# Making the low part of every fourth weight tile by an accumulating transfer instead of a VectorE subtraction

## The chip, the cores and the metric

The kernel runs on one core of a Trainium2 chip. The metric is the device time of one execution in microseconds (us), as the median of several runs; less is better. The engines are named as the profile names them: PE is TensorE (matrix products; PEld are its weight loads), DVE is VectorE, ACT is ScalarE, POOL is GpSimd, SP is SyncE, which here only issues transfers. A "q" behind an engine's name means its instruction sequencer. Besides these, 16 DMA engines move data between HBM and the on-chip memory.

## The reference

One layer of an encoder over 256 positions of width 2048, all in float32. Cut to its matrix products:

```python
hn = rms_norm(h, g_mix_pre);  u = hn @ w_in                     # 2048 x 5120
q, k, v, xr, yg = split(u)
attn = neighborhood_attention(q, k, v, rpb)
rec = rglru_bidirectional(xr, ...) * gelu(yg)
mixed = concat([rms_norm(attn), rms_norm(rec)]) @ w_out         # 2048 x 2048
h = h + rms_norm(mixed, g_mix_post)
fn = rms_norm(h, g_ffn_pre)
ff = (silu(fn @ w_ffn_gate) * (fn @ w_ffn_up)) @ w_ffn_down     # 2048 x 5632, twice, and back
h = h + rms_norm(ff, g_ffn_post)
gate = sigmoid(rms_norm(h, g_ple_pre) @ w_ple_gate)             # 2048 x 2048
h = h + rms_norm(gate * (p @ w_ple_proj), g_ple_post)           # 256 x 2048
```

## The kernel before

**Split products.** Each float32 operand is held as two numbers of the narrower type fp32r (`F32R`): a high part, which is the value rounded, and a low part, which is the value less its high part. A product is three matmuls into one float32 accumulator: high by high, high by weight-low, low by weight-high (lines 390, 391, 392 in `products`).

**Weight tiles.** All weights are cut into 412 tiles of 128 partitions by 2 by 512 float32 numbers (512 KB each, 4 KB per partition), listed in `tiles` in the order of use: 80 for `w_in` (0 to 79), then `w_out`, two of `w_ple_proj`, the feed-forward weights, two more of `w_ple_proj`, and 32 for `w_ple_gate`. Each tile takes twelve matmuls of 512 columns on PE. A tile goes through four steps, numbered by tile `i`:

- `load_stream` (line 339): SP issues the transfer of the raw tile from HBM into `wr`. There are four such buffers (`R_BUFS`), used in turn, so tile `i` takes the buffer of tile `i-4`, and its transfer waits until that buffer was last read.
- `hi_stream` (line 362): ACT copies `wr` into `wh`, which rounds it. `wh` and `wl` have four buffers each (`W_BUFS`), so the copy of tile `i` waits for the last matmul of tile `i-4`.
- `lo_stream` (line 372): DVE writes `wl = wr - wh`. It is the last reader of `wr`.
- `products` (lines 390 to 392): PE uses `wh` in the first matmul of the tile and `wl` in the second.

The first tile is loaded in two halves, and the last eight tiles keep their buffers for a second pass, four of them in buffers of their own (`bw`).

**The order of the work.** Every engine runs its instructions in the order in which the program issues them. That order comes from a planner (`Plan`): each stream is a generator that yields the engine it needs next and an estimated cost, and the planner keeps a clock for each engine and issues whatever can start first, in time before PE needs it. `act(n)`, `dve(n)` and `dma(kb)` are such costs; `take` and `give` count buffers, and an `Event` holds the planned time at which something is done. The planner's clocks only set the order. On the chip each instruction waits by semaphores for what it reads and for the buffer it writes.

POOL issues no transfer in this kernel: it only clears buffers and makes constants.

Of the kernel before, what the change touches and what calls it, by code (L numbers as in the profile page):

```python
# [12 lines left out]
AF = mybir.ActivationFunctionType  # L13
ALU = mybir.AluOpType
# [13 lines left out]
N = 512  # L28
# [25 lines left out]
R_BUFS = 4  # L54
SM_BUFS = 4
LATE = 0.8


class Event:
# [5 lines left out]
class Task:  # L65
    def __init__(self, gen, ready, late):
        self.gen, self.ready, self.sure, self.late, self.op = gen, ready, ready, late, None


class Plan:  # L70
# [11 lines left out]
    MARGIN = 0.4  # L82

    def __init__(self, **slots):
        self.clk = {"act": 0.0, "dve": 0.0, "pe": 0.0, "dma": 0.0}
        self.free = {k: [0.0] * n for k, n in slots.items()}
        self.tables = None
        self.tasks = []
        self.now = 0.0
# [97 lines left out]
def act(n, tables=COPY, take=None, give=None):  # L187
    return ("act", 0.15 + 0.00082 * n, tables, take, give)


def dve(n, take=None, give=None):
    return ("dve", 0.08 + 0.00104 * n, None, take, give)


def pe(cost, take=None, give=None):
    return ("pe", cost, None, take, give)


def dma(kb, take=None):
# [4 lines left out]
def layer(ctx: ExitStack, tc: tile.TileContext, a: dict, out: bass.AP):  # L204
    nc = tc.nc
# [4 lines left out]
    plan = Plan(wr=R_BUFS, w=W_BUFS, sm=SM_BUFS, ev=1, mid=2, bt=2)  # L210

    def f32(t):
        return t.bitcast(F32)
# [41 lines left out]
    def transposed(e, b0):  # L255

        yield pe(0.44, take="sm")
        tr = bank("tr")
        for b in range(2):
            for t in range(NT):  # L260
                sl = slice((b0 + b) * P, (b0 + b + 1) * P)
                nc.tensor.transpose(tr[:, b, t * P : (t + 1) * P], e[:, t, sl], ident)  # L262
        return tr
# [13 lines left out]
    def done(event):  # L277
        event.t = plan.now
# [32 lines left out]
    tiles = []  # L311
# [7 lines left out]

    raws, his, los = {}, {}, {}  # L320
    ev_raw, ev_hi, ev_lo = {}, {}, {}
    extra_loads = {}
    big_w = {}

    def pieces(i):

        return [slice(0, 1), slice(1, 2)] if i == 0 else [slice(0, 2)]
# [16 lines left out]
    def lateness(at):  # L344

        return LATE if at[0] - at_pe[0] >= 2 else -LATE

    def hi_stream():
        for i in range(len(tiles)):
            at_hi[0] = i  # L350
            for j in pieces(i):
                n = j.stop - j.start
                yield ev_raw[i, j.stop]
                if i in big_w:
                    yield big_w[i][2]
                yield act(n * N, take=None if j.start or i in big_w else "w")
                if i in big_w:
                    his[i], los[i] = big_w[i][0](), big_w[i][1]()
                elif not j.start:
                    his[i] = wp.tile([P, 2, N], F32R, tag="wh", name="wh")  # L360
                    los[i] = wp.tile([P, 2, N], F32R, tag="wl", name="wl")
                nc.scalar.copy(his[i][:, j, :], raws[i][:, j, :])  # L362
                done(ev_hi[i, j.stop])

    def lo_stream():
        for i in range(len(tiles)):
            at_lo[0] = i
            for j in pieces(i):
                n = j.stop - j.start
                yield ev_hi[i, j.stop]  # L370
                yield dve(n * N, give="wr" if j.stop == 2 else None)
                nc.vector.tensor_tensor(  # L372
                    out=los[i][:, j, :], in0=raws[i][:, j, :], in1=f32(his[i][:, j, :]),
                    op=ALU.subtract,
                )
                done(ev_lo[i, j.stop])
            raws.pop(i)
# [82 lines left out]
    def make_hT(odd):  # L460
        for k in range(odd, KD // 2, 2):
            for j in range(2):
                b = 2 * k + j
                yield ev_xs[b]
                yield from gained_split(
                    hT_hi[:, b, :], hT_lo[:, b, :], xs[k][:, j, :], col("g_mix_pre", b)
                )
                done(hT.ev[b])
# [4 lines left out]
    def norm_x():  # L473
        ss = const.tile([P, NT, 2], F32, name="ss_x")
        for i in range(2 * NT):
            t, c = i // 2, i % 2
            v = xn[t][:, c * DA : (c + 1) * DA]
            yield ev_xn[i]
            yield act(DA)
            nc.scalar.activation(v, v, AF.Square, accum_out=ss[:, t, c : c + 1])  # L480
        tot = const.tile([P, NT], F32, name="tot_x")
        yield dve(64)
        nc.vector.tensor_reduce(out=tot, in_=ss, op=ALU.add, axis=AX.X)
        yield from rstd_of(tot, D, rstd_x, const.tile([P, NT], F32, name="rt_x"))
        done(ev_x)
# [137 lines left out]
    def rec_unit(b0, xp):  # L623
# [24 lines left out]
        for i, (dst, bn) in enumerate(((r, "b_rg_a"), (ig, "b_rg_i"))):  # L648
            pg = [None] * 2
            for z in range(2):  # L650
                yield pe(0.66, take="sm")
                pg[z] = bank("pg")
                for c in range(2):
                    w = 4 * z + 2 * i + c
                    mm3(pg[z][:, c, :], gh[:, w, :], gl[:, w, :], xch[:, c, :], xcl[:, c, :],
                        True, True)
            for z in range(2):
                for c in range(2):
                    yield act(S, SIG, give="sm" if c else None)
                    nc.scalar.activation(  # L660
                        dst[:, z, c, :], pg[z][:, c, :], AF.Sigmoid, bias=col(bn, z * 8 + b0 + c)
                    )
                if i:
                    plan.add(gate_input(z, gated[z]), plan.now)
# [55 lines left out]
    def group_rstd(ss, name):  # L720

        yield pe(0.44, take="sm")
        pb = bank(f"pb_{name}")
        nc.tensor.matmul(pb[:, 0, :], ones, ss, start=True, stop=True)
        rb = const.tile([P, S], F32, name=f"rb_{name}")
        yield act(S, SQRT, give="sm")
        nc.scalar.activation(rb, pb[:, 0, :], AF.Sqrt, bias=eps, scale=1.0 / DA)
        yield dve(S)
        nc.vector.reciprocal(rb, rb)
        return rb  # L730
# [592 lines left out]
    for i in range(len(tiles)):  # L1323
        for j in pieces(i):
            for ev in (ev_raw, ev_hi, ev_lo):
                ev[i, j.stop] = Event()
    i0 = segs[-1][-1]
    keep.update(range(i0, i0 + 8))
    bw = {}
# [12 lines left out]

    plan.add(load_stream())
    plan.add(hi_stream(), late=lambda: lateness(at_hi))
    plan.add(lo_stream(), late=lambda: lateness(at_lo))
    plan.add(make_hT(0), late=-2 * LATE)
    plan.add(make_hT(1), late=-2 * LATE)
    plan.add(norm_x())
# [77 lines left out]
```

## Time and profile before

| | us |
|---|---|
| median of 2 runs (1197.97 and 1198.37) | 1198.17 |
| span of the profiled execution, first to last instruction | 1195.1 |
| PE busy within the span | 1176.7 |
| DVE busy | 695.1 |
| ACT busy | 635.0 |
| POOL busy | 1.6 |

The profile is of one execution. What lies around its span isn't in the trace: its own time is not listed apart from the runs', whose median stands 3.1 us above the span. The granted TensorE clock of the core was 0.997 of full speed. Matmuls are pipelined, so the duration of one (0.39 us) is longer than the distance from one to the next, and "busy" is the time in which at least one is under way.

A line of a group reads: source line, engine, operation, tiles written and read, shape, count, then busy time, mean duration of one in ns, idle time of the engine just before these instructions, and what ended that idle time. A line of the timeline reads: start in us from the span's start, duration in us, engine, line, operation, tiles.

### The profile page before, as it was taken

Reading aid. Unit: us, or ns where it says so; the run is one execution under the profiler, and the core shown is the slowest. Engines: PE = TensorE matmul, PEld = TensorE weight load, DVE = VectorE, ACT = ScalarE, POOL = GpSimd, SP = SyncE. Lnnn points to the kernel's source line nnn. Section 1 sums busy time; section 2 is a strip of 40 time slices with the busy share of each in tenths; the row PEclk is TensorE's granted clock in tenths of the full one; section 3 lists DMA queues with packets and bytes.
Section 4 is the critical chain, followed back from the end, with each engine's and each line's share of the span. In section 5 each row is a group of like instructions: output and inputs, shape, how many; then the busy total and the mean of one; then the engine's idle time right before and its main releaser. Section 6 shows DMA issues by size and latency. Waiting matters only on the chain.

```text
span 1195.1 us, 14294 instructions
## 1 busy us (share of the span) xinstructions
PE 1176.7 (98%) x5388; PEld 975.7 (82%) x5388; DVE 695.1 (58%) x823; ACT 635.0 (53%) x842; POOL 1.6 (0%) x13
## 2 busy tenths in 40 slices
PE   7999999999999999999999999999999999999996
PEld 5888888888888888888888888888888888888885
DVE  5676867877557545545444544545454544657664
ACT  6787776766457344344444444443334444446753
POOL 0000000000000000000000000000000000000000
PEclk9999999999999999999999999999999999999998
DMA  8765566545865666566666566565666666565661
GB/s 305 234 213 186 154 197 188 172 160 183 314 196 195 191 193 183 190 193 187 193 194 193 186 193 191 184 194 187 193 194 194 189 184 194 175 208 177 218 222 72
DMA packets 69205, 232.23 MB, mean 194 GB/s; under 512 B 7440, under 2 KB 13456, under 8 KB 68496
## 3 DMA queue, kind: packets, MB, share of 16 engines
q1 hardware_dynamic: 68992, 231.24, 61.2%
q8 instruction: 42, 0.69, 0.2%
q14 instruction: 27, 0.22, 0.1%
q10 hardware_dynamic: 144, 0.08, 0.0%
HBM read 229.19 MB, written 2.10 MB: 194 GB/s over the span
## 4 chain that ended last, share of the span: by engine, by line
PE 98%; DVE 1%; ACT 0%; DMA 0%; SPq 0%; issue 0%; DVEq 0%
PE acc L392 31%; PE acc L390 31%; PE acc L391 31%; PE tr L262 2%; DMA xs<-in_xT 0%; PE pg L267 0%; PE pg L268 0%; PE pg L266 0%; PE tr L877 0%; DVE wl L372 0%; DVE h L1310 0%; PE po L268 0%; PE sc L267 0%; PE sc L268 0%; PE po L267 0%; PE po L266 0%
## 5 line engine op out<-in xcount | busy, mean ns | idle before, releaser
L372 DVE TENSOR_TENSOR wl<-wr,wh 128x1024 fp32r<-128x1024 f32 (+1 forms) x409 | 497.2, 1221 | 379.4 <-ACT wh L362 379.1
L362 ACT CAST wh<-wr 128x1024 fp32r<-128x1024 f32 (+1 forms) x409 | 428.7, 1050 | 471.5 <-PE acc L392 451.5
L390 PE MATMUL acc<-wh,hT_mix_hi 128*128 128x512 f32 x704 | 275.8, 392 | 0.0
L392 PE MATMUL acc<-wh,hT_mix_lo 128*128 128x512 f32 x704 | 274.3, 390 | 0.3 <-DVE hT_mix_lo L251 0.3
L391 PE MATMUL acc<-wl,hT_mix_hi 128*128 128x512 f32 x704 | 274.0, 389 | 0.0
L392 PEld LDWEIGHTS acc<-wh,hT_mix_lo 128*128 128x128 f32 x704 | 132.1, 188 | 28.5 <-DVE hT_mix_lo L251 0.9
L391 PEld LDWEIGHTS acc<-wl,hT_mix_hi 128*128 128x128 f32 x704 | 132.2, 188 | 26.9
L390 PEld LDWEIGHTS acc<-wh,hT_mix_hi 128*128 128x128 f32 x704 | 132.2, 188 | 26.6
L390 PE MATMUL acc<-wh,hT_hi 128*128 128x512 f32 x320 | 127.9, 400 | 6.9 <-ACT wh L362 6.9
L391 PE MATMUL acc<-wl,hT_hi 128*128 128x512 f32 x320 | 125.7, 393 | 1.4 <-DVE wl L372 1.4
L392 PE MATMUL acc<-wh,hT_lo 128*128 128x512 f32 x320 | 125.5, 392 | 0.0
L390 PEld LDWEIGHTS acc<-wh,hT_hi 128*128 128x128 f32 x320 | 60.6, 189 | 18.5 <-ACT wh L362 6.9
L391 PEld LDWEIGHTS acc<-wl,hT_hi 128*128 128x128 f32 x320 | 60.4, 189 | 14.7 <-DVE wl L372 3.2
L392 PEld LDWEIGHTS acc<-wh,hT_lo 128*128 128x128 f32 x320 | 60.3, 189 | 12.9
L390 PE MATMUL acc<-wh,mid0h 128*128 128x512 f32 x128 | 50.0, 390 | 0.0
L390 PE MATMUL acc<-wh,mid1h 128*128 128x512 f32 x128 | 50.0, 390 | 0.0
L392 PE MATMUL acc<-wh,mid0l 128*128 128x512 f32 x128 | 49.8, 389 | 0.0
L392 PE MATMUL acc<-wh,mid1l 128*128 128x512 f32 x128 | 49.8, 389 | 0.0
L391 PE MATMUL acc<-wl,mid0h 128*128 128x512 f32 x128 | 49.8, 389 | 0.0
L391 PE MATMUL acc<-wl,mid1h 128*128 128x512 f32 x128 | 49.8, 389 | 0.0
L390 PE MATMUL acc<-wh,hT_ffn_hi 128*128 128x512 f32 x112 | 44.1, 394 | 0.0
L392 PE MATMUL acc<-wh,hT_ffn_lo 128*128 128x512 f32 x112 | 43.7, 390 | 0.0
(231 smaller groups left out, 1308.4 us busy)
## 6 DMA issues: line engine op xcount, KB each, us to landing
wr<-in_w_ffn_gate SPq DMA_DIRECT2D x88, 512.0 KB, 4.2
wr<-in_w_ffn_up SPq DMA_DIRECT2D x88, 512.0 KB, 4.2
wr<-in_w_ffn_down SPq DMA_DIRECT2D x88, 512.0 KB, 4.3
wr<-in_w_in SPq DMA_DIRECT2D x79, 512.0 KB, 4.3
wr<-in_w_out SPq DMA_DIRECT2D x32, 512.0 KB, 4.6
wr<-in_w_ple_gate SPq DMA_DIRECT2D x32, 512.0 KB, 4.2
xn<-in_x SPq DMA_DIRECT2D x4, 512.0 KB, 6.2
h<-in_x SPq DMA_DIRECT2D x2, 1024.0 KB, 8.1
```

The costliest lines, as they stand in the source:

```text
L262: nc.tensor.transpose(tr[:, b, t * P : (t + 1) * P], e[:, t, sl], ident)
L362: nc.scalar.copy(his[i][:, j, :], raws[i][:, j, :])
L372: nc.vector.tensor_tensor(out=los[i][:, j, :], in0=raws[i][:, j, :], in1=f32(his[i][:, j, :]), op=ALU.subtract,)
L390: nc.tensor.matmul(accs[t], hi[:, sl], wh[:, j, :], start=st, stop=False)
L391: nc.tensor.matmul(accs[t], hi[:, sl], wl[:, j, :], start=False, stop=False)
L392: nc.tensor.matmul(accs[t], lo[:, sl], wh[:, j, :], start=False, stop=sp)
```

## The change

For tiles with `i % 4 == 3`, from tile 19 to tile 403 (97 tiles), the DVE subtraction is left out. ACT, after its copy to `wh`, writes the negated high part into `wl` by a second instruction. Then POOL issues a transfer that adds the raw weights onto `wl`. For every other one of these tiles (`i % 8 == 3`, 49 of them) the raw weights are read from `wr`, on the chip; for the others (48) they are read from HBM a second time. The planner gets one more clock, `sum`, with a cost of 5.0 for each such transfer. DVE's stream skips these tiles.

```diff
+SUM_EVERY = 4
...
-        self.clk = {"act": 0.0, "dve": 0.0, "pe": 0.0, "dma": 0.0}
+        self.clk = {"act": 0.0, "dve": 0.0, "pe": 0.0, "dma": 0.0, "sum": 0.0}
...
+def summed(give=None):
+    return ("sum", 5.0, None, None, give)
...
+    ev_neg = {}
+
+    def by_transfer(i):
+        return i % SUM_EVERY == SUM_EVERY - 1 and 16 <= i < len(tiles) - 8
...
                 nc.scalar.copy(his[i][:, j, :], raws[i][:, j, :])
                 done(ev_hi[i, j.stop])
+                if by_transfer(i):
+                    yield act(n * N)
+                    nc.scalar.activation(los[i], f32(his[i]), AF.Copy, scale=-1.0)
+                    done(ev_neg[i])
+                    plan.add(sum_tile(i), plan.now)
+
+    def sum_tile(i):
+        yield summed(give="wr")
+        if i % (2 * SUM_EVERY) == SUM_EVERY - 1:
+            src = raws[i]
+        else:
+            w, k, n0 = tiles[i]
+            src = a[w][n0 // N, k // 2]
+        nc.gpsimd.dma_start(los[i], src, accum_op=ALU.add)
+        done(ev_lo[i, 2])
+        raws.pop(i)
 
     def lo_stream():
         for i in range(len(tiles)):
+            if by_transfer(i):
+                continue
```

More of the change, by code (lines that the diff above doesn't have):

```diff
@@ L1326, in layer @@
                 ev[i, j.stop] = Event()
+        ev_neg[i] = Event()
     i0 = segs[-1][-1]
```

## The prediction

> **What bounds the kernel now.** I read the page's shares of the engines first, then the chain of waits, then the waits of PE, then the groups of the two steps that the change touches.
>
> ```profile
> PE 1176.7 (98%) x5388; PEld 975.7 (82%) x5388; DVE 695.1 (58%) x823; ACT 635.0 (53%) x842; POOL 1.6 (0%) x13
> ...
> PE 98%; DVE 1%; ACT 0%; DMA 0%; SPq 0%; issue 0%; DVEq 0%
> ...
> L372 DVE TENSOR_TENSOR wl<-wr,wh 128x1024 fp32r<-128x1024 f32 (+1 forms) x409 | 497.2, 1221 | 379.4 <-ACT wh L362 379.1
> L362 ACT CAST wh<-wr 128x1024 fp32r<-128x1024 f32 (+1 forms) x409 | 428.7, 1050 | 471.5 <-PE acc L392 451.5
> ```
>
> ```profile
> PE acc L390 <- ACT wh L362: 6.9, 1, 6.9
> PE acc L391 <- DVE wl L372: 1.4, 2, 0.7
> PE acc L392 <- DVE hT_mix_lo L251: 0.3, 1, 0.3
> ```
>
> PE is the bound: 98% of the span and 98% of the chain. The streams wait for PE (the ACT cast waited 451.5 us for a matmul to free its buffer) and not the other way round: in the whole run PE matmuls waited 1.4 us for DVE's low parts. So the 97 subtractions that go, 97 x 1.221 = 118 us of DVE, lie wholly beside PE's work; what they can give back is those 1.4 us. Even PE's whole idle time, 1195.1 - 1176.7 = 18.4 us, is 1.5% of the span. The question is only whether the new way of making a low part still ends before PE asks for it.
>
> **The room of one tile.** The timeline in the middle of the feed-forward stage shows it:
>
> ```profile
> 600.53 0.39 PE L392 MATMUL acc<-wh,mid0l 128*128 128x512 f32 x1
> 600.96 1.05 ACT L362 CAST wh<-wr 128x1024 fp32r<-128x1024 f32 x1 [1.67 <-PE acc L392]
> 602.05 1.22 DVE L372 TENSOR_TENSOR wl<-wr,wh 128x1024 fp32r<-128x1024 f32 x1 [1.49 <-ACT wh L362]
> 603.30 0.33 SPq L339 DMA_DIRECT2D wr<-in_w_ffn_down  x1
> 608.92 0.39 PE L390 MATMUL acc<-wh,mid0h 128*128 128x512 f32 x1
> 609.15 0.39 PE L391 MATMUL acc<-wl,mid0h 128*128 128x512 f32 x1
> 611.84 1.05 ACT L362 CAST wh<-wr 128x1024 fp32r<-128x1024 f32 x1 [1.67 <-PE acc L392]
> ```
>
> The matmul at 600.53 is the last of some tile; it ends at 600.92 and frees its buffers. The cast of the tile four later starts at 600.96, its subtraction ends at 603.27, and SP then issues the load into the freed raw buffer at 603.30. PE has three tiles in hand: it starts on ours at 608.92 and first needs its low part at 609.15. So a low part has 609.15 - 600.96 = 8.19 us from the start of its cast; the subtraction uses 2.31 of them. The cast at 611.84 is that of the tile four further on: 2.69 us after the low part was first used.
>
> **Part by part.** *Subtraction out:* at most 1.4 us gained, counted as nothing. *Negation on ACT:* one instruction of 128 x 1024 for each of 97 tiles. The nearest row, among the groups, has that shape; the row below it is of the busy times by stretch, in the order PE, PEld, DVE, ACT, POOL:
>
> ```profile
> L480 ACT ACTIVATE xn<-xn 128x1024 f32<-128x1024 f32 x4 | 4.2, 1062 | 1.4 <-DMA xn<-in_x 1.1
> ```
>
> ```profile
> 40.00:160.00 120.00, 120.00 (x611) 101.65 (x610) 90.44 (x154) 93.70 (x149) 0.00 (x0) 1.00 0.60 187
> ```
>
> 97 x 1.06 = 103 us, on an engine that is 53% busy, and 78% (93.70 of 120) in the attention stage. Behind it on ACT stand the next tile's cast and the copies out of the accumulators; each comes up to 1.06 us later, against the 8.19 - 2.31 = 5.9 us that a plain tile has to spare, so I count nothing for it. If that cover were gone it would cost 1 us for each such tile, 97 x 1.06. In the sum tile itself the negation ends 1.09 (cast start to the next engine's start) + 1.06 = 2.15 us after the cast began, which leaves the transfer L = 8.19 - 2.15 = 6.0 us.
>
> *The transfer on POOL's queue:* no row shows one, nor an addition in a transfer. Behind a waiting one on POOL stand only later ones. Its duration L, from the end of the negation to the semaphore that PE waits for, is the unknown; the nearest rows are transfers of SP's queue, 512 KB and 1 MB, and the page's queue line:
>
> ```profile
> DMA to landing us min/median/max: 2.7/4.3/9.3
> ```
>
> ```profile
> xn<-in_x SPq DMA_DIRECT2D x4, 512.0 KB, 6.2
> h<-in_x SPq DMA_DIRECT2D x2, 1024.0 KB, 8.1
> ...
> gain_g_mix_post<-in_g_mix_post SPq DMA_DIRECT2D x1, 1024.0 KB, 6.5
> gain_g_ffn_post<-in_g_ffn_post SPq DMA_DIRECT2D x1, 1024.0 KB, 7.8
> gain_g_ple_post<-in_g_ple_post SPq DMA_DIRECT2D x1, 1024.0 KB, 4.5
> ```
>
> ```profile
> q1 hardware_dynamic: 68992, 231.24, 61.2%
> ```
>
> The first line is for the raw weight loads: 512 KB in 4.3 us at the median. The queue line prices one pass of a tile through the 16 engines: 0.612 x 1195.1 us x 16 / 68992 packets = 0.170 us a packet, and 128 packets over 16 engines make 1.36 us. An addition has to read two operands, so at least one pass more: 4.3 + 1.36 = 5.7 us. Taken as the transfer of 1 MB that it amounts to, the five rows have a median of 7.8. I take the middle, L = 6.7; the ends are 4.3 (the addition costs nothing over a load) and 9.3 (the longest load).
>
> [...]
>
> *The raw buffer:* this is the second, tighter limit. The waits of SP's queue show what its loads stand behind:
>
> ```profile
> SPq L339 <- DVE wl L372: 927.1, 397, 8.2
> ```
>
> All loads but a few wait for a subtraction to free a buffer. Where the transfer reads `wr` (49 tiles), the load of tile A+4 waits for the transfer of tile A, and every later load waits behind it in SP's queue. Tile A+4 is itself made by transfer (from HBM; its raw buffer is free after the cast). So pairs of these tiles chain: cast and negation 2.15, transfer L, load 4.3, cast and negation 2.15, transfer L, and 2.69 from the first use of the low part to the cast of A+8. That is 2L + 11.3 us for eight tiles. What PE needs for eight tiles comes from the number of casts by stage:
>
> ```profile
> 47.00:254.00 207.00, 66.50 (x64) 1.00 0.56 175
> 254.00:360.00 106.00, 40.03 (x38) 1.00 0.69 231
> 360.00:1060.00 700.00, 266.23 (x253) 1.00 0.62 191
> 1060.00:1154.00 94.00, 35.03 (x35) 1.00 0.63 197
> ```
>
> From 254 to 1154 us: 900 us for 326 tiles, 2.76 each, 22.1 for eight. In the `w_in` stage (47 to 254), where PE has other work too, 207 / 64 = 3.23, or 25.9. So the chain is longer than PE's work where L is over (22.1 - 11.3) / 2 = 5.4 us after 254 us, and over 7.3 before. With L = 6.7 a pair takes 24.7 us, 2.6 more than PE needs; tiles 80 to 403 hold 40.5 pairs: 105 us. The 8 pairs of `w_in` fit.
>
> The DMA engines themselves suffice: 97 x 2 passes x 1.36 = 264 us on top of 0.612 x 1195.1 = 731, 995 in all.
>
> **Sum.** 1195.1 + 105 = 1300 as a span; the runs' median stands 3.1 us above the profiled span, so 1303 us. Each us on L costs 81 us up to 7.3, 97 beyond.
>
> **The rivals.** *Hidden (not slower).* The mechanism is the prefetch: with L at 5.4 or less both limits hold, PE never waits, and the time is 1198, or 1196 with the 1.4 us. It decides at L = 5.4; up to 5.7 (5.7 gives 2 x 5.7 + 11.3 - 22.1 = 0.6 a pair, 24 us) it still counts as no change. For it: the load's median of 4.3, and the 1 MB row at 4.5. Against it: 5.7 is the sum with one extra pass and no price for the issue. Chance 0.25.
>
> *Slow addition.* If the engines need four passes, as for elements read, added and written back one after the other, L = 4.3 + 3 x 1.36 = 8.4: a pair takes 28.1, so 40.5 x 6.0 + 8 x 2.2 = 261 us, 1459. For it: 8.1 us for 1 MB; against it: the loads' median. At the end of 9.3 it is 29.9 a pair, 40.5 x 7.8 + 8 x 4.0 = 348 us, 1546. Chance 0.22.
>
> *Held up by DVE.* If the transfer's issue had to wait out a subtraction under way, 1.22 us, L = 7.9 and a pair takes 27.1: 40.5 x 5.0 + 8 x 1.2 = 212, 1410. DVE is busy for 58% of the span, so about half of the transfers would meet one. Chance 0.04. [...]
>
> *Faster by over 2%* would take 24 us, more than PE's idle 18.4. Chance 0.01.
>
> **The numbers.** The forecast case, L from 5.7 to 7.8, has 0.48. 2% of 1198 is 24 us, which I take as about what a measurement can tell from no change. Faster 0.01, within 0.25, slower 0.22 + 0.04 + 0.48 = 0.74. Forecast alone: 1222 (L = 5.7) to 40.5 x 4.8 + 8 x 1.0 = 202 more, 1400 (L = 7.8). The range takes in the hidden case below, 1196, and the end of 9.3 above, 1546; what is left out is mostly an L beyond 9.3, about 0.1.
>
> **What would show it.** Right: PE waits at L391 for a transfer into `wl`, in total about 105 us, at most one long wait for eight tiles, on the tiles that read HBM; SP's loads wait for transfers into `wl`; landings of POOL's transfers at 6 to 7.5 us; ACT up by 103 us and DVE down by 118; casts that wait for a late `wr`. Wrong in size: landings below 5.4 (no wait, 1198) or above 7.8. Wrong in mechanism: PE waiting at L390 for casts on other tiles, waits on both kinds of sum tiles alike with raw tiles early (then the raw buffer isn't the limit, and only L above 6.0 counts), or waits behind ACT's longer queue in the attention stage.

## The result

1288.81 us (median of 2 runs, 1285.41 and 1292.2) against 1198.17 before: a ratio of 1.0759, with a 95% interval of 1.0691 to 1.0827. The profiled execution took 1285.41 us, with a span of 1283.6: 88.5 us more than the 1195.1 of before.

### The profile page after: what moved, and what is told of

Read it like the earlier page. It is cut to its first block, busy times and chain, and to the rows that moved or that the text cites. A ratio compares the mean times of both kernels' runs of the same rounds, so it can differ in the third digit from the quotient of the medians.

```text
span 1283.6 us, 14518 instructions
## 1 busy us (share of the span) xinstructions
PE 1202.7 (94%) x5388; PEld 981.7 (76%) x5388; DVE 581.7 (45%) x726; ACT 727.9 (57%) x935; POOL 85.5 (7%) x110
## 4 chain that ended last, share of the span: by engine, by line
PE 45%; DMA 18%; ACT 6%; issue 2%; DVE 2%; DVEq 0%; ACTq 0%
PE acc L418 15%; PE acc L419 15%; PE acc L417 14%; DMA wl<-in_w_ffn_down 5%; DMA wl<-in_w_ffn_up 5%; DMA wl<-in_w_ffn_gate 4%; ACT wl L375 3%; ACT wh L371 2%; DMA wl<-wr 1%; DMA wl<-in_w_out 1%; DMA wl<-in_w_ple_gate 1%; PE tr L267 1%; DVE h L1124 1%; DVE hT_ffn_lo L256 0%; ACT junk L1135 0%
## 5 line engine op out<-in xcount | busy, mean ns | idle before, releaser
L371 ACT CAST wh<-wr 128x1024 fp32r<-128x1024 f32 (+1 forms) x409 | 428.3, 1048 | 452.3 <-PE acc L419 419.4
L399 DVE TENSOR_TENSOR wl<-wr,wh 128x1024 fp32r<-128x1024 f32 (+1 forms) x312 | 379.8, 1220 | 542.5 <-ACT wh L371 542.0
L418 PE MATMUL acc<-wl,hT_mix_hi 128*128 128x512 f32 x704 | 277.2, 394 | 18.4 <-DMA wl<-in_w_ffn_gate 9.1
L417 PE MATMUL acc<-wh,hT_mix_hi 128*128 128x512 f32 x704 | 276.9, 393 | 0.0
L419 PE MATMUL acc<-wh,hT_mix_lo 128*128 128x512 f32 x704 | 275.2, 391 | 0.0
L418 PEld LDWEIGHTS acc<-wl,hT_mix_hi 128*128 128x128 f32 x704 | 132.7, 188 | 53.2 <-DMA wl<-in_w_ffn_up 12.9
L419 PEld LDWEIGHTS acc<-wh,hT_mix_lo 128*128 128x128 f32 x704 | 132.6, 188 | 27.2 <-DVE hT_mix_lo L256 0.2
L417 PEld LDWEIGHTS acc<-wh,hT_mix_hi 128*128 128x128 f32 x704 | 132.6, 188 | 27.2
L418 PE MATMUL acc<-wl,hT_hi 128*128 128x512 f32 x320 | 127.3, 398 | 11.2 <-DMA wl<-in_w_in 10.5
L417 PE MATMUL acc<-wh,hT_hi 128*128 128x512 f32 x320 | 128.4, 401 | 6.9 <-ACT wh L371 6.9
L419 PE MATMUL acc<-wh,hT_lo 128*128 128x512 f32 x320 | 126.3, 395 | 0.0
L375 ACT ACTIVATE wl<-wh 128x1024 fp32r<-128x1024 f32 x97 | 103.0, 1061 | 2.5
L386 POOL DMA_DIRECT2D wl<-wr x49 | 42.3, 863 | 632.0 <-ACT wl L375 548.9
L418 PEld LDWEIGHTS acc<-wl,hT_hi 128*128 128x128 f32 x320 | 60.9, 190 | 27.9 <-DMA wl<-in_w_in 13.7
L417 PEld LDWEIGHTS acc<-wh,hT_hi 128*128 128x128 f32 x320 | 61.0, 191 | 18.7 <-ACT wh L371 6.9
L419 PEld LDWEIGHTS acc<-wh,hT_lo 128*128 128x128 f32 x320 | 60.8, 190 | 12.6
L418 PE MATMUL acc<-wl,mid0h 128*128 128x512 f32 x128 | 50.3, 393 | 6.8 <-DMA wl<-in_w_ffn_down 6.8
L418 PE MATMUL acc<-wl,mid1h 128*128 128x512 f32 x128 | 50.9, 398 | 5.4 <-DMA wl<-in_w_ffn_down 5.4
L417 PE MATMUL acc<-wh,mid1h 128*128 128x512 f32 x128 | 50.7, 396 | 0.0
L418 PE MATMUL acc<-wl,hT_ffn_hi 128*128 128x512 f32 x112 | 45.2, 404 | 5.6 <-DMA wl<-wr 2.9
L419 PE MATMUL acc<-wh,mid1l 128*128 128x512 f32 x128 | 50.4, 394 | 0.0
L417 PE MATMUL acc<-wh,mid0h 128*128 128x512 f32 x128 | 50.0, 391 | 0.0
```

What stands on the lines that cost most here:

```text
L375: nc.scalar.activation(los[i], f32(his[i]), AF.Copy, scale=-1.0)
L386: nc.gpsimd.dma_start(los[i], src, accum_op=ALU.add)
L399: nc.vector.tensor_tensor(out=los[i][:, j, :], in0=raws[i][:, j, :], in1=f32(his[i][:, j, :]), op=ALU.subtract,)
L417: nc.tensor.matmul(accs[t], hi[:, sl], wh[:, j, :], start=st, stop=False)
L418: nc.tensor.matmul(accs[t], hi[:, sl], wl[:, j, :], start=False, stop=False)
L419: nc.tensor.matmul(accs[t], lo[:, sl], wh[:, j, :], start=False, stop=sp)
```

## The profile after

The additions of the diff move the lines: the cast is now L371, the negation L375, the adding transfer L386, the subtraction L399, and the three matmuls L417 to L419. The loads are L348. First the page: shares of the engines, the costliest groups that answer to those of before, the queues.

```profile
PE 1202.7 (94%) x5388; PEld 981.7 (76%) x5388; DVE 581.7 (45%) x726; ACT 727.9 (57%) x935; POOL 85.5 (7%) x110
...
q1 hardware_dynamic: 68992, 231.24, 53.5%
q0 software_dynamic: 13968, 50.86, 22.8%
...
PE 45%; DMA 18%; ACT 6%; issue 2%; DVE 2%; DVEq 0%; ACTq 0%
...
L371 ACT CAST wh<-wr 128x1024 fp32r<-128x1024 f32 (+1 forms) x409 | 428.3, 1048 | 452.3 <-PE acc L419 419.4
L399 DVE TENSOR_TENSOR wl<-wr,wh 128x1024 fp32r<-128x1024 f32 (+1 forms) x312 | 379.8, 1220 | 542.5 <-ACT wh L371 542.0
...
L375 ACT ACTIVATE wl<-wh 128x1024 fp32r<-128x1024 f32 x97 | 103.0, 1061 | 2.5
L386 POOL DMA_DIRECT2D wl<-wr x49 | 42.3, 863 | 632.0 <-ACT wl L375 548.9
```

DVE lost 113 us of work, ACT gained 93 (the negations alone are 103.0; four loads of function tables fewer, 5.1 us, are part of the difference), and PE, still the bound, is idle for 80.9 us instead of 18.4. The chain of waits now runs through transfers for 18% of the span. The waits of PE name them (tiles written and read, us in total, times, longest):

```profile
PE acc L418 <- DMA wl<-in_w_ffn_down: 16.1, 9, 2.1
PE acc L418 <- DMA wl<-in_w_out: 10.7, 4, 5.4
PE acc L418 <- DMA wl<-in_w_in: 10.5, 8, 2.2
PE acc L418 <- DMA wl<-in_w_ffn_gate: 9.1, 7, 2.1
PE acc L418 <- DMA wl<-in_w_ffn_up: 8.7, 9, 2.0
PE acc L417 <- ACT wh L371: 6.9, 1, 6.9
PE acc L418 <- DMA wl<-wr: 5.3, 5, 2.9
PE acc L418 <- DMA wl<-in_w_ple_gate: 2.7, 2, 2.0
```

Leaving out the start-up wait for a cast, which was there before, these are 63.1 us, the whole of PE's new idle time. All but 5.3 us is for transfers that read HBM. The issues by source show what sets these apart (size, median us from POOL's start to landing):

```profile
wl<-wr POOLq DMA_DIRECT2D x49, 512.0 KB, 4.6
...
wl<-in_w_ffn_gate POOLq DMA_DIRECT2D x11, 512.0 KB, 7.0
wl<-in_w_ffn_up POOLq DMA_DIRECT2D x11, 512.0 KB, 6.2
wl<-in_w_ffn_down POOLq DMA_DIRECT2D x11, 512.0 KB, 7.5
wl<-in_w_in POOLq DMA_DIRECT2D x8, 512.0 KB, 7.3
```

Two kinds of transfer: from the chip 4.6 us, from HBM about 7. The timeline of one pair in the feed-forward stage (tile 187 reads the chip, tile 191 HBM):

```profile
598.50 0.86 POOL L386 DMA_DIRECT2D wl<-wr  x1 [11.91 <-ACT wl L375]
601.07 0.33 SPq L348 DMA_DIRECT2D wr<-in_w_ffn_down  x1
603.15 0.33 SPq L348 DMA_DIRECT2D wr<-in_w_ffn_down  x1
604.20 0.39 PE L418 MATMUL acc<-wl,mid0h 128*128 128x512 f32 x1
606.93 1.05 ACT L371 CAST wh<-wr 128x1024 fp32r<-128x1024 f32 x1 [1.71 <-PE acc L419]
608.01 0.33 SPq L348 DMA_DIRECT2D wr<-in_w_ffn_down  x1
608.02 1.06 ACT L375 ACTIVATE wl<-wh 128x1024 fp32r<-128x1024 f32 x1
609.38 0.87 POOL L386 DMA_DIRECT2D wl<-in_w_ffn_down  x1 [10.02 <-ACT wl L375]
614.85 0.39 PE L417 MATMUL acc<-wh,mid0h 128*128 128x512 f32 x1
617.21 0.50 PE L418 MATMUL acc<-wl,mid0h 128*128 128x512 f32 x1 [1.97 <-DMA wl<-in_w_ffn_down]
```

Tile 187's transfer starts at 598.50 and lands 4.6 us later, at 603.1; PE wants it at 604.20 and waits for nothing. Tile 191's cast starts 10.88 us after that of 187 (four tiles of PE work, nothing late), its negation ends at 609.08, POOL starts 0.3 us later, and PE asks 8.15 us after the cast, at 615.08. The transfer lands only at 617.17, and PE waits 2 us. Three things about the loads are to be seen. The load at 601.07 is that of tile 191: it goes out while the transfer of 187 is still reading its raw buffer, so it took another buffer, the one that the subtraction of tile 188 had freed. The load at 603.15 is that of tile 192, and goes out as soon as the transfer has landed. And the load at 608.01 goes out as the cast of 191 ends: nothing holds that tile's raw buffer any more, since its transfer reads HBM, so this load runs beside the slow transfer.

## The experiments

Two theories of the slow kind stood against each other, and the recorded chain through the raw buffer as a third. **C**: the slow transfers share the DMA engines with weight loads, which the fast kind holds back by keeping its raw buffer. **S**: reading HBM makes them slow. **R**: the chain.

**All from the chip.**

```diff
-        if i % (2 * SUM_EVERY) == SUM_EVERY - 1:
+        if True:
```

> All 97 low parts are added from the raw buffer on the chip, none from HBM. Theory C (the slow transfers are slow because weight loads share the DMA engines with them; a transfer that reads wr keeps its raw buffer busy and so holds the next loads back): all 97 land 4.6 to 5.2 us after POOL starts them, inside the room, PE waits under 20 us for wl in total, time 1198 to 1215. Theory S (reading HBM is what makes a transfer slow): the same, 1198 to 1215. Theory R (the recorded chain: the load four tiles later waits for the transfer): 2.15 + 4.9 + 4.4 = 11.45 us from cast to cast of these tiles against 11.0, some 0.45 x 81 = 36 us, about 1235.

1229.44 us, ratio 1.0262 (1.0246 to 1.0277). The median landing is 4.6 us for all 97, but the sum is above what C and S gave. To see where, I took the time from the first matmul of one tile to that of another in each trace, and subtracted that of before (us):

```
tiles from   16     80    116    140    220    300    372
to           80    116    140    220    300    372    404
changed   +13.2  +16.2   +4.9  +14.7  +12.3  +13.9  +12.4
all chip   +4.6  +15.8   +3.0    0.0   +0.3   +0.3   +6.5
```

From tile 140 to 371, the feed-forward stage, the cost is gone: 0.6 us instead of 41. R would have taken 0.45 us for each of 58 tiles there, 26 us: R is out, and that its total of 1235 came near was chance. What is left lies in the crowded stages, in a few long waits. Measured from the start of a tile's first matmul to that of its second, less the usual 0.23 us, ten tiles wait over 0.2 us, 20 us together. The transfers land alike, after 4.6 us at the median, on the tiles that read the chip before and on those that read HBM, so the tile's place in the cycle of eight is not what made the two kinds. The longest is tile 95's, here in the timeline of this kernel (SP's issues, POOL's, and PE around the wait):

```profile
307.07 0.38 SPq L1020 DMA_DIRECT2D gain_g_mix_post<-in_g_mix_post  x1
307.51 0.43 SPq L1028 DMA_DIRECT2D pw<-in_pT  x1
307.98 0.46 SPq L1032 DMA_DIRECT2D h<-in_x  x1
310.97 0.86 POOL L386 DMA_DIRECT2D wl<-wr  x1 [11.01 <-ACT wl L375]
315.00 0.39 PE L417 MATMUL acc<-wh,rec_hi 128*128 128x512 f32 x1
321.19 0.79 PE L418 MATMUL acc<-wl,rec_hi 128*128 128x512 f32 x1 [5.80 <-DMA wl<-wr]
```

This transfer, from the chip, is issued 3 us after 2.25 MB of other loads, and lands 10.2 us after its start. So a transfer can be slow without reading HBM. The same tile waits 5.4 us in the changed kernel, where it reads HBM.

**All from HBM.**

```diff
-        if i % (2 * SUM_EVERY) == SUM_EVERY - 1:
+        if False:
```

> All 97 low parts are added from HBM. C and S alike: all transfers land about 7.1 us after POOL's start, PE waits about 1.4 us at each of 97 tiles, twice the 72 us of the changed kernel, plus more stretches at half clock: 1340 to 1375. R (no raw buffer is held any more, so the chain is gone): about 1198.

1338.27 us in one run, just below the range of C and S. Median landing 6.9 us; 82 of the 97 tiles wait. R's 1198 fails here too.

**From the chip, with the raw buffer free early.**

```diff
-            src = a[w][n0 // N, k // 2]
+            src = f32(his[i])
```

> The 48 transfers that read HBM read the tile's own high part on the chip instead, so the low part of these tiles is left out (it becomes zero); the raw buffer is still free after the cast, and the loads come as early as before. C: landing 6.5 us or more after POOL's start, PE waits 50 us or more, time 1265 to 1290. S: landing 4.6 to 5.0, no waits, time 1198 to 1212.

1239.23 us in one run: neither. The 48 transfers that now read `wh` land in 5.6 us at the median, the 49 others in 4.6 as before (issues by source):

```profile
wl<-wr POOLq DMA_DIRECT2D x49, 512.0 KB, 4.6
wl<-wh POOLq DMA_DIRECT2D x48, 512.0 KB, 5.6
```

In the trace, 268 packets of loads (a tile is 128) start between the start and the landing of such a transfer (median), against 54 for one that reads `wr`. Loads beside it thus cost 1.0 us; that the two kinds also read different buffers of the chip was not tested apart.

**From HBM, with the raw buffer held.**

```diff
+    hold = const.tile([P, 1], F32, name="hold")
...
+        if i % (2 * SUM_EVERY) != SUM_EVERY - 1:
+            nc.gpsimd.tensor_tensor(
+                out=hold, in0=raws[i][:, 0, 0:1], in1=f32(los[i])[:, 0, 0:1], op=ALU.add
+            )
```

> The 48 transfers still read HBM, but a one-column POOL addition that reads wr and wl after the transfer keeps the raw buffer busy until it has landed, so that the next load waits as it does for the other 49. C: landing falls from 7.1 to 4.6 to 5.5 us, PE waits under 25 us, time 1198 to 1220. S: landing stays near 7, PE still waits, time 1280 or more.

1234.45 us, ratio 1.0303 (1.0281 to 1.0326). The edit does hold loads back: 98 packets of them start during a transfer from HBM (median), against 292 in the changed kernel. Landing from HBM falls from 7.1 to 5.5 us, as C had it; the time stays above C's range, for the crowded stages again (3.4 us are lost from tile 140 to 371). Its issues by source:

```profile
wl<-wr POOLq DMA_DIRECT2D x49, 512.0 KB, 4.8
wl<-in_w_ffn_gate POOLq DMA_DIRECT2D x11, 512.0 KB, 5.5
wl<-in_w_ffn_up POOLq DMA_DIRECT2D x11, 512.0 KB, 5.5
```

Together: from the chip with few loads beside it 4.6; from the chip beside more loads 5.6; from HBM with most loads held back 5.5; both, 7.1, somewhat more than the two additions of 1.0 and 0.9 make. Room after POOL's start is 8.15 - 2.44 = 5.7 us (cast to use, less cast to POOL's start). At the median each cause by itself fits; only both together don't.

**The transfer left out.**

```diff
-        nc.gpsimd.dma_start(los[i], src, accum_op=ALU.add)
```

> The transfer is left out: the low part of the 97 tiles is only the negated high part, the raw weights are not added. What is left of the change is ACT's second instruction and the subtraction that is gone. If the transfers are all of the cost: 1196 to 1202. If ACT's 103 us matter in the crowded stages (rival): 1205 to 1225, with PE waits around tiles 51, 83, 95, 123 and 387 as in the kernel with all sums on the chip.

1197.58 us, ratio 0.9993 (0.9984 to 1.0002). The whole cost is the transfers'. ACT's 103 us cost nothing, and DVE's 118 us give nothing, with the interval at 0.2% either way.

**Only the feed-forward stage, from the chip and mixed.** Both set the tiles so; the first also takes all sums from the chip.

```diff
-        return i % SUM_EVERY == SUM_EVERY - 1 and 16 <= i < len(tiles) - 8
+        return i % SUM_EVERY == SUM_EVERY - 1 and 140 <= i < 372
```

> All sums read the raw buffer, and only tiles 140 to 371 are made so (58 of them), where ACT and DVE have little else and no other large loads run. If the transfer is hidden there, as the kernel with all sums on the chip showed within 0.6 us over these tiles: 1197 to 1201, no difference from before, and 71 us of DVE time saved for nothing. If the hidden cost was only put off to the stages that follow: 1205 or more.

1200.42 us, ratio 1.0015 (1.0006 to 1.0024), within the expected range: hidden, with 58 subtractions fewer. Over tiles 140 to 371 it is 0.8 us longer than before; the rest of the 1.9 us lies outside and wasn't traced to a cause.

> As the changed kernel (every other sum reads HBM), but only tiles 140 to 371. The changed kernel lost 41 us over these tiles: 1236 to 1242 if stage costs add up; 1198 if the slow transfers of this stage come from what the crowded stages before it left behind.

1244.58 us in one run, just above the range where stage costs add up. Over these tiles 44.6 us are lost, 34 of them waits of its 29 tiles that read HBM. The slow kind needs no crowded stage before it.

**The addition left out, the transfer kept.**

```diff
-        nc.gpsimd.dma_start(los[i], src, accum_op=ALU.add)
+        nc.gpsimd.dma_start(los[i], src)
```

> The transfers of the changed kernel without the addition: a plain copy of the raw weights over the negated high part, so the low part of 97 tiles is the raw weight. If the addition costs its second pass (328 ns a packet against 159): landing falls by about 1.4 us, to 3.3 on the chip and 5.5 to 5.9 from HBM, which is inside the room of 5.7 us left after POOL's start for most tiles: 1205 to 1230. If the price is the queue and the source and not the addition: landings within 0.4 us of 4.6 and 7.1, and 1275 or more.

1210.89 us in one run, inside the first range; the landings fell by more than expected (3.3 from the chip, 5.5 to 5.9 from HBM). Landings and the queue's line:

```profile
q0 software_dynamic: 13968, 50.86, 12.2%
...
wl<-wr POOLq DMA_DIRECT2D x49, 512.0 KB, 2.9
wl<-in_w_ffn_gate POOLq DMA_DIRECT2D x11, 512.0 KB, 4.2
wl<-in_w_ffn_up POOLq DMA_DIRECT2D x11, 512.0 KB, 4.8
wl<-in_w_ffn_down POOLq DMA_DIRECT2D x11, 512.0 KB, 4.8
```

0.122 x 1209.1 / 97 = 1.52 us of all 16 engines for a copy; with the addition 0.228 x 1283.6 / 97 = 3.02. The addition costs as much engine time again, 1.5 us, and 1.7 us of landing from the chip; from HBM beside loads it costs 1.4 to 2.8, and why more was not tested.

## Why the prediction was right, and where not

The forecast of 1303 stands 14 us above the median, and its sign and case held. That it came so near is in part luck: one step of its mechanism failed, and its errors cancel. By its steps:

- *PE bounds, and the subtraction out is worth nothing:* right, shown by the run without the transfer (0.9993).
- *The negation costs nothing on ACT:* right, by the same run; 1061 ns each, as the row of 1062 had it.
- *The room, 6.0 us after the negation:* right. Tile 191 asked 8.15 us after its cast, against 8.19 as read before; POOL takes 0.3 us of it before it starts.
- *The transfer, L = 6.7 for all:* the mean was near and the shape wrong. With POOL's 0.3 us, L was 4.9 from the chip and 7.4 from HBM, 6.2 on average. The second pass, 1.36 us by the load's packets, measured 1.5. What I had no term for is that source and loads add up (4.6 us with neither, 5.5 and 5.6 with one, 7.1 with both). (The "five rows" with a median of 7.8 were four rows of 1 MB, of five transfers; the median of the rows is 7.2.)
- *The raw buffer as the tighter limit, 2L + 11.3 for a pair:* this step failed. It rested on the load of tile A+4 waiting for A's transfer. In the trace that load went out 2 us before the landing, into the buffer that the subtraction of A+1 had freed. In the kernel before, the four raw buffers are used in turn; in the changed one they are not: in the feed-forward stage the load of A+4 took the buffer of A+1 for every one of these tiles. It is the load of A+5 that waits for the transfer (at 603.15). Both had time: at the median the raw tile of A+4 had landed 2.2 us before its cast, and that of A+5 2.3. With the measured 4.9 + 7.4 the formula gives 23.6 against 22.1, 1.5 us a pair, and the wait at an HBM tile is 7.4 - 6.0 = 1.4: two mechanisms with nearly the same sum. The run with all sums on the chip parts them, 0.6 us against 26. Even so the total came out by luck: with the measured L the formula gives 40.5 x 1.5 = 61 us and not 105. The guess of 6.7, half a microsecond too long, stood in for what the sum left out, above all the 13 us in `w_in` and the clock's 11.
- *Nothing lost in `w_in`:* wrong by 13 us. PE takes 25.9 us for a pair there, more than the formula's 24.7, but the limit that counted is the one of the single tile, and its room is little longer in that stage (8.6 us from cast to use at the median, against 8.1). All eight tiles that read HBM there wait, 1.0 to 2.3 us each.
- *What would show it:* PE waits at L418 for `wl`, at most one long wait for eight tiles and on those that read HBM: so it was (40 of 48 wait over 0.2 us, 6 of the other 49), with 63 us in total and not 105. SP's loads waited for transfers into `wl`, 122 us in 49 waits. Landings at 6 to 7.5 us: only the HBM kind. Casts late for `wr`: hardly any. Of the recorded signs of a wrong mechanism, raw tiles early came true; waits on both kinds alike did not, because L differed by kind.
- *The rivals:* "hidden" is what the tiles from the chip did in the feed-forward stage, and what the change would have been without the second read of HBM there. "Slow addition" with four passes didn't show: 3.02 us of engine time against 1.52 for a copy are two. "Held up by DVE" didn't show: its 1.22 us are the length of one subtraction, and no run showed an issue that waits for it. In the changed kernel a subtraction into `wl` was under way while POOL issued for 14 of the 97 transfers, not for half of them, and POOL's part was 0.86 to 0.88 us in 13 of these and 1.01 in one, against a mean of 0.87 over all.

Of the 88.5 us, 62.5 are PE idle. Another 11, by an estimate, are the clock, below. Of the other 15, about 9 are the edges of waits: a matmul's record (0.39 us) is longer than the distance to the next (0.23), so measured from start to start the waits for transfers come to 72 us against 63. The rest I have not taken apart.

## What to carry to other kernels

Work taken off an engine that PE never waits for was worth nothing here, 118 us of it; look for what the replacement puts between a buffer's release and its use, and compare its latency with that room, not its bandwidth. An accumulating transfer took twice the engine time of a copy here (3.02 us against 1.52), and its latency depended on its source and on what else was in flight (4.6 to 7.1 us): to give its source buffer back early cost more here than it gave, since the next load then ran beside it (1288.81 us, against 1234.45 with the buffer held). When two mechanisms predict nearly the same total, only a run that changes one of them tells which is at work.

## What the runs showed of the hardware

Waits of PE cost more than their length here. Tile 95 in the changed kernel waits from 321.4 to 327.1; after it the matmuls start 0.43 us apart instead of 0.23, and take 0.63 us. The timeline, and the busy times by stretch (PE, PEld, DVE, ACT, POOL, then the granted clock, the DMA engines' share and GB/s):

```profile
321.37 0.39 PE L417 MATMUL acc<-wh,rec_hi 128*128 128x512 f32 x1
327.13 0.80 PE L418 MATMUL acc<-wl,rec_hi 128*128 128x512 f32 x1 [5.37 <-DMA wl<-in_w_out]
...
329.00 0.63 PE L419 MATMUL acc<-wh,rec_lo 128*128 128x512 f32 x1
329.43 0.63 PE L417 MATMUL acc<-wh,rec_hi 128*128 128x512 f32 x1
```

```profile
314.90:321.30 6.40, 6.40 (x30) 5.31 (x29) 2.66 (x4) 4.11 (x6) 0.87 (x1) 1.00 1.01 366
327.10:333.00 5.90, 5.87 (x15) 4.64 (x16) 0.72 (x2) 1.33 (x5) 0.00 (x0) 0.55 0.93 385
```

The clock records show stretches at half speed (0.50 granted) around the end of such a wait: in the changed kernel five of 3.4 us, and one of 6.8 at tile 95, which begins at 325.54, 1.6 us before the wait ends. Over the traces of the changed kernel and the first four experiments: none after 42 idle gaps of PE of over 1 and up to 1.5 us, 8 after 42 of 1.5 to 2.2, 17 after 23 of 2.2 us or more. The start-up wait of each trace, 6.5 to 7.3 us, is left out of these; no such stretch began within 6 us of its end. In the changed kernel these stretches, with one of 7.8 us at the kernel's end, make 31.7 us against 9.2 before, all of that at the kernel's end, which at half speed loses about (31.7 - 9.2) / 2 = 11 us, an estimate. The shortest gap of the changed kernel with such a stretch after it was 1.80 us (it ends at 1133.22, the stretch begins at 1134.50); gaps of 2.17 and 2.67 us, which end at 104.78 and 378.16, had none.
